# Two transformer stacks on one core: unread transposes ahead of the first product, the first x tile by the scalar queue, the last norm's sums by products, results by two queues

## The chip, the core and the metric

One core of a Trainium2 chip runs the whole program in one launch. The metric is device time in microseconds (us), from three runs. Engines are named as in the profile: PE does matrix products and transposes and writes PSUM banks, PEld is PE's weight load, DVE and ACT do elementwise work, POOL does a little of it, SP only starts transfers. A transfer's data is moved by 16 DMA engines that all queues share; "SPq" and "ACTq" rows are the moments at which SP and ACT issue one.

## What is computed

The program runs two stacks of two layers each over 256 tokens of 1024 features: the first has attention, a short convolution and a gated network per layer, the second has modulated norms, a mixer of three branches and two gated networks per layer. All products are float32. The parts that matter here are the very first product and the very last norm:

```
proj = jnp.einsum('bsd,de->bse', x, w_in)           # the first product, x is [1, 256, 1024]
...
def rms_norm(x, g):                                  # the last operation, over 1024 features
    xf = x.astype(jnp.float32)
    y = xf * lax.rsqrt(jnp.mean(xf * xf, axis=-1, keepdims=True) + EPS)
    return (y * g.astype(jnp.float32)).astype(x.dtype)
```

## The kernel before, in words

Activations lie feature-major: a tile holds two blocks of 128 features by 256 tokens. Each float32 operand is split into a high and a low part, `hi` by ACT (a rounding copy, line 302) and `lo` by DVE (the rest, lines 261 and 305), and a product of two float32 operands is three products on PE, high by high, low by high and high by low (`mm3`, line 373 in `mm`).

**Weights** come as 765 chunks of 512 KB, in the order in which PE uses them (`Weights`). A chunk holds eight 128x128 tiles, so it feeds 8 x 3 = 24 products of 256 columns. It is loaded into one of six `raw` buffers by an SP transfer (line 242), then split by ACT into `wh` and by DVE into `wl`, of which there are six each. A `raw` buffer is free again when DVE has made `wl`. Loads are issued as far ahead as the buffers allow, splits four chunks ahead.

**Start** (`setup`, line 495 on). SP issues in turn the four tiles of x (`x`, 256 KB each) and the first four weight chunks, then the vectors, the distance table and two conditioning rows `cb`. POOL fills `ones768` and builds the identity `ident` that every transpose on PE needs. The transfer of `rope` on ACT's queue is written much later in the program (line 526) but stands first on ACT, because nothing holds it back. A layer under the kernel records the whole program, orders each engine's instructions and sets the waits. It gives transfers eight semaphores in turn, so a ninth transfer is issued when the one eight places earlier has landed.

The first products (`g`, in `mixer1`) run over the feature blocks outermost: chunk 0 uses the first block of x, and eight chunks fill four PSUM banks. Then ACT copies one of those banks out (`qk`), and PE makes attention logits from the copy (`lg`). On ACT, between the splits of the chunks and that copy, stand a table load and the activation of `cb`.

**End** (`block2`, line 1776 on). The last gated network adds into `h[0]` tile by tile. After each tile ACT squares it (`sq`, line 302 from `rms_add`), and the squares of the first seven blocks are added up in one tile `q`; the eighth stays apart as `last`. `rms_root` calls `colsum` (line 476): four transposes on PE put `q` and `last` token-major into a PSUM bank, and DVE adds each row up. Seven small DVE instructions (`rsqrt`) make the inverse root `rs`. Meanwhile ACT multiplies each of the eight blocks with the gain (`hg`), PE transposes each to token-major (`tr`, line 1785), two banks for each half of the tokens. Last, two DVE and two ACT instructions scale the four banks with `rs` into `out` tiles of 256 KB, and SP issues the four result transfers (line 1793).

Of the kernel before, what the change touches and what calls it, by code (L numbers as in the profile page):

```python
# [10 lines left out]
F32 = mybir.dt.float32  # L11
# [4 lines left out]
ALU = mybir.AluOpType  # L16
# [3 lines left out]
P = 128  # L20
D = 1024
# [258 lines left out]
class Kernel:  # L280
# [212 lines left out]
    def setup(self):  # L493
        nc, sb = self.nc, self.sb
        a = self.aps
        self.w = Weights(self, a["w"], self.NSPLIT - 2, 6)

        self.xs_raw = [self.slot("x") for _ in range(4)]
        for j in range(4):
            nc.sync.dma_start(self.xs_raw[j], a["x"][:, 2 * j:2 * j + 2, :])  # L500
            self.w.load(j + 1)
        nv = a["vecs"].shape[1]
        self.vecs = sb.tile([P, nv], F32, name="vecs")
        self.ident = sb.tile([P, P], F32, name="ident")
        self.ones768 = sb.tile([P, P], F32, name="ones768")
        nc.gpsimd.memset(self.ones768, 1.0 / 768)
        make_identity(nc, self.ident)
        nc.sync.dma_start(self.vecs, a["vecs"])
        self.dist = sb.tile([P, 2, 384], F32, name="dist")
        nc.sync.dma_start(self.dist, a["dist"].rearrange("p (a b) -> p a b", a=2))  # L510
        self.rope = sb.tile([P, T], F32, name="rope")
        self.dft_h = sb.tile([P, 768], F32R, name="dft_h")
        self.dft_l = sb.tile([P, 768], F32R, name="dft_l")
        self.cb = sb.tile([P, 2, D], F32, name="cb")
        nc.sync.dma_start(self.cb[:, 0, :], a["c"].partition_broadcast(P))
        nc.sync.dma_start(self.cb[:, 1, :], a["c_ctx"].partition_broadcast(P))
        self.mods = sb.tile([P, DEPTH, 2, NADA], F32, name="mods")
        self.convpad = sb.tile([P, 3, T + 32], F32, name="convpad")
        nc.gpsimd.memset(self.convpad, 0.0)
        self.cpad = [sb.tile([P, T + 2], F32, name=f"cpad{j}") for j in range(2)]  # L520
        for j in range(2):
            nc.gpsimd.memset(self.cpad[j], 0.0)
# [1178 lines left out]
    def block2(self, h_lat):  # L1701
        self.h = [h_lat, None]
        h = self.h
        self.roots = {}
        for l in range(DEPTH):
            last = l == DEPTH - 1
            got = {}
            if l == 0:
                self.rms_all(0)
                us = self.normed(0, 0)  # L1710
                self.ffn_early(3, self.et)
                h[1] = self.load_ctx()
            else:
                self.norm_both(0, 0)
                us = list(zip(*self.u))
                self.u = None
            for s in range(2):
                self.rms_begin(s)

            self.ada_plan(l, 24, 72, ADA[3]) if l else self.ada_plan(l, 24, 72, ADA[4], ADA[5])  # L1720
            if l:
                self.ada_gate(l, 0)

            def ctx_done():
                self.ada_ready(l, 1)
                got["c"] = self.normed(1, 1)

            if l == 0:
                uc, self.uc = self.uc, None
                self.ffn_rest(f"a{l}", us, uc, self.ffn2_add(0, h, (0, 1)), ctx_done)  # L1730
                self.early = None
            else:
                self.ffn_both(f"a{l}", us, self.ffn2_add(0, h, (0, 1)), ctx_done)
            del us

            self.layer_vectors(l)
            def lat_norm():
                got["x"] = self.normed(0, 1)

            if not last:  # L1740
                self.sides.append(self.root_side(0))
                kctx, vctx = self.mixer2(l, 1, got.pop("c"), h[1], None, None, lat_norm)
                rest = lambda: None
            else:
                lat_norm()
                kctx, vctx, rest = self.ctx_keys(l, got.pop("c"))

            def ctx_norm():
                self.u = self.both_operands("u")
                self.norm_both(1, 2)  # L1750

            if not last:
                self.sides.append(self.root_side(1))
            self.mixer2(l, 0, got.pop("x"), h[0], kctx, vctx, (lambda: None) if last else ctx_norm, rest)
            del kctx, vctx, rest
            if not last:
                self.ada_plan(1, 0, 24, ADA[2])
                self.norm_both(0, 2)
                us = list(zip(*self.u))
                self.u = None  # L1760

                def next_ctx():
                    self.ada_ready(1, 0)
                    self.u = self.both_operands("u")
                    self.norm_both(1, 0)

                for s in range(2):
                    self.rms_begin(s)
                self.ffn_both(f"b{l}", us, self.ffn2_add(2, h, (0, 1)), next_ctx)
                del us  # L1770
            else:
                us = self.normed(0, 2)
                add = self.ffn2_add(2, h, (0,))
                self.rms_begin(0)
                self.ffn_single("c", us, 2, lambda m, psum, last: add(0, m, psum, last))
        y = self.rms_root(0, D)
        g = self.vec("g_final_2", 0)
        banks = [[self.bank("mm", "tr") for _ in range(2)] for _ in range(2)]
        for k in range(KD):
            if k % 2 == 0:  # L1780
                t = self.slot("hg")
            self.act(t[:, k % 2, :], h[0][k // 2][:, k % 2, :], AF.Copy, scale=g[:, k:k + 1])
            for b in range(2):
                o = banks[b][k // 4].rearrange("p a b -> p (a b)")[:, (k % 4) * P:(k % 4 + 1) * P]
                self.nc.tensor.transpose(o, t[:, k % 2, b * P:(b + 1) * P], self.ident)
        for j in range(2):
            for b in range(2):
                t = self.slot("out")
                if b:
                    self.act(t, banks[b][j], AF.Copy, scale=y[:, b:b + 1])  # L1790
                else:
                    self.ts(t, banks[b][j], y[:, b:b + 1], None, ALU.mult)
                self.nc.sync.dma_start(self.aps["out"][b * P:(b + 1) * P, j * 512:(j + 1) * 512],
                                       t.rearrange("p a b -> p (a b)"))


# [45 lines left out]
```

## Time and profile before

| | us |
|---|---|
| median of three runs | 2903.86 (2903.77 to 2904.89) |
| the profiled execution, its own time | 2903.97 |
| its span, first to last instruction | 2902.2 |
| outside the span | 1.77 |
| PE busy | 2866.9 (99% of the span) |
| first product starts at | 7.28 |
| first result transfer issued at | 2897.01 |

The profile is one execution. Section 1 of its page gives busy time by engine; the view of waits gives, for each engine, what ended its idle time; the timeline gives start, length, engine, line, operation and operands, with the idle time just before in brackets; the table by stretch gives busy time, granted clock of PE, mean busy share of the DMA engines and GB/s.

### The profile page before, as it was taken

Reading aid. Unit: us, or ns where it says so; the run is one execution under the profiler, and the core shown is the slowest. Engines: PE = TensorE matmul, PEld = TensorE weight load, DVE = VectorE, ACT = ScalarE, POOL = GpSimd, SP = SyncE. Lnnn points to the kernel's source line nnn. Section 1 sums busy time; section 2 is a strip of 40 time slices with the busy share of each in tenths; the row PEclk is TensorE's granted clock in tenths of the full one; section 3 lists DMA queues with packets and bytes.
Section 4 is the critical chain, followed back from the end, with each engine's and each line's share of the span. In section 5 each row is a group of like instructions: output and inputs, shape, how many; then the busy total and the mean of one; then the engine's idle time right before and its main releaser. Section 6 shows DMA issues by size and latency. Waiting matters only on the chain. (4 is left out here: it accounts for less than half of the span.)

```text
span 2902.2 us, 49995 instructions
## 1 busy us (share of the span) xinstructions
PE 2866.9 (99%) x20172; PEld 2648.9 (91%) x20172; DVE 2084.9 (72%) x3565; ACT 1356.8 (47%) x2171; POOL 112.1 (4%) x121
## 2 busy tenths in 40 slices
PE   8999999999999999999999999999999999999999
PEld 7999899899999999999999998888888888899998
DVE  7879778648767787798878875555765556887554
ACT  6645545744554432257557643222322223675443
POOL 1001001000001000010010000000100001000000
PEclk9999999999999999999999999999999999999999
DMA  7565655354654764544453443333354443435452
GB/s 280 195 228 178 221 202 174 133 186 150 210 187 160 240 218 167 172 155 153 165 178 117 153 167 131 138 131 116 114 184 167 167 159 113 162 112 175 160 183 101
DMA packets 134440, 486.30 MB, mean 168 GB/s; under 512 B 14912, under 2 KB 15168, under 8 KB 134208
## 3 DMA queue, kind: packets, MB, share of 16 engines
q1 hardware_dynamic: 133776, 482.58, 48.1%
q8 instruction: 158, 2.59, 0.4%
q14 instruction: 74, 0.61, 0.1%
q10 hardware_dynamic: 432, 0.52, 0.1%
HBM read 482.00 MB, written 1.05 MB: 166 GB/s over the span
## 5 line engine op out<-in xcount | busy, mean ns | idle before, releaser
L302 ACT ACTIVATE wh<-raw 128x1024 fp32r<-128x1024 f32 x765 | 808.1, 1058 | 1127.8 <-issue 180.9
L261 DVE TENSOR_TENSOR wl<-raw,wh 128x1024 fp32r<-128x1024 f32 x765 | 939.3, 1230 | 454.7 <-ACT wh L302 443.1
L547 DVE SCALAR_TENSOR_TENSOR junk<-ada,cb 128x1024 bf16<-128x1024 f32 x256 | 313.4, 1224 | 3.1 <-DMA ada<-in_w_ada_dram 1.1
L373 PE MATMUL f<-x,wh 128*128 128x512 f32 (+1 forms) x832 | 243.4, 359 | 0.0
L373 PE MATMUL f<-x,wl 128*128 128x256 f32 x704 | 185.1, 280 | 0.0
L373 PE MATMUL bg<-wh,wh 128*128 128x256 f32 x576 | 168.0, 292 | 0.0
L373 PE MATMUL bg<-wh,wl 128*128 128x256 f32 x576 | 163.4, 284 | 0.0
L373 PE MATMUL bg<-wl,wh 128*128 128x256 f32 x576 | 162.9, 283 | 0.0
L373 PEld LDWEIGHTS f<-x,wh 128*128 128x128 f32 x832 | 142.9, 188 | 19.7 <-DVE fm L305 0.2
L373 PE MATMUL b<-uh,wl 128*128 128x512 f32 (+1 forms) x384 | 145.8, 380 | 0.0
L373 PE MATMUL a<-uh,wh 128*128 128x512 f32 (+1 forms) x384 | 145.3, 379 | 0.0
L1214 POOL TENSOR_TENSOR sq<-sq,sq 128x256 f32<-128x256 f32 x63 | 64.3, 1028 | 2097.8 <-ACT sq L302 2075.4
L373 PE MATMUL a<-wh,wh 128*128 128x256 f32 x512 | 144.8, 283 | 0.0
L373 PE MATMUL a<-wl,wh 128*128 128x256 f32 x512 | 144.6, 282 | 0.0
L373 PE MATMUL b<-ul,wh 128*128 128x512 f32 (+1 forms) x384 | 144.3, 376 | 0.0
L373 PE MATMUL a<-uh,wl 128*128 128x512 f32 (+1 forms) x384 | 144.2, 376 | 0.0
L373 PE MATMUL a<-ul,wh 128*128 128x512 f32 (+1 forms) x384 | 143.7, 374 | 0.0
L373 PE MATMUL a<-wh,wl 128*128 128x256 f32 x512 | 143.7, 281 | 0.0
L373 PE MATMUL b<-uh,wh 128*128 128x512 f32 (+1 forms) x384 | 143.6, 374 | 0.0
L373 PEld LDWEIGHTS f<-x,wl 128*128 128x128 f32 x704 | 131.8, 187 | 6.2
L308 DVE SCALAR_TENSOR_TENSOR cva<-convpad,wdw,cva 128x256 f32<-128x256 f32 x270 | 126.9, 480 | 3.0
L373 PEld LDWEIGHTS bg<-wh,wh 128*128 128x128 f32 x576 | 108.7, 189 | 4.3 <-issue 4.1
(452 smaller groups left out, 8424.5 us busy)
## 6 DMA issues: line engine op xcount, KB each, us to landing
raw<-in_w_dram SPq DMA_DIRECT2D x765, 512.0 KB, 3.3
ada<-in_w_ada_dram SPq DMA_DIRECT2D x144, 512.0 KB, 4.2
hc<-in_ctx_dram SPq DMA_DIRECT2D x8, 256.0 KB, 5.4
x<-in_x_dram SPq DMA_DIRECT2D x4, 256.0 KB, 5.9
out_dram<-out SPq DMA_DIRECT2D x4, 256.0 KB, 2.4
cb<-in_c_dram SPq DMA_DIRECT2D x1, 512.0 KB, 8.6
cb<-in_c_ctx_dram SPq DMA_DIRECT2D x1, 512.0 KB, 8.2
dist<-in_dist_dram SPq DMA_DIRECT2D x1, 384.0 KB, 7.9
```

Source lines behind the costliest of these rows:

```text
L261: self.last_split = kb.nc.vector.tensor_tensor(lo.rearrange("p a b -> p (a b)"), raw, f.bitcast(F32), ALU.subtract)
L302: return self.nc.scalar.activation(out, in_, func, **kw)
L308: return self.nc.vector.scalar_tensor_tensor(out, a, s, b, op0, op1)
L373: return self.nc.tensor.matmul(out, a, b, start=start, stop=stop)
L547: self.nc.vector.scalar_tensor_tensor(junk, raw, 1.0, self.cb[:, s, :], ALU.mult, ALU.mult, accum_out=self.mods[:, l, s, c:c + 1])
L1214: self.nc.gpsimd.tensor_tensor(r["q"], r["q"], q[:, 0, :], ALU.add)
```

## The change

Four edits, two at each end of the program; the order of everything between is the same on all engines.

1. The first tile of x is issued by ACT, not by SP.
2. POOL makes the identity first, and PE then does 20 transposes of the identity into a bank that is not read.
3. The last norm's sums are made by four products of `q` and `last` (as weights) with a column of ones, which leave the sums of 128 tokens in one column each; DVE's row sum is gone, and the small DVE chain reads PSUM.
4. Of the four result transfers, the two that ACT's `out` tiles feed are issued by ACT.

```diff
         for j in range(4):
-            nc.sync.dma_start(self.xs_raw[j], a["x"][:, 2 * j:2 * j + 2, :])
+            (nc.sync if j else nc.scalar).dma_start(self.xs_raw[j], a["x"][:, 2 * j:2 * j + 2, :])
             self.w.load(j + 1)
...
+        make_identity(nc, self.ident)
+
+        idle = self.bank("st", "idle").rearrange("p a b -> p (a b)")
+        for _ in range(20):
+            nc.tensor.transpose(idle[:, :P], self.ident, self.ident)
         nc.gpsimd.memset(self.ones768, 1.0 / 768)
-        make_identity(nc, self.ident)
+        self.one = sb.tile([P, 1], F32, name="one")
+        nc.gpsimd.memset(self.one, 1.0)
...
-        y = self.rms_root(0, D)
+        r = self.rms.pop(0)
+        st = self.bank("st", "fs")
+        for b in range(2):
+            for j, x in enumerate(("q", "last")):
+                self.mm(st[:, b, 0:1], r[x][:, b * P:(b + 1) * P], self.one, j == 0, j == 1)
+        v = self.small("v")
+        self.ts(v, st[:, :, 0], -1.0 / D, -1e-6, ALU.mult, ALU.add)
+        y = self.rsqrt(v)
...
-                self.nc.sync.dma_start(self.aps["out"][b * P:(b + 1) * P, j * 512:(j + 1) * 512],
+                (self.nc.scalar if b else self.nc.sync).dma_start(self.aps["out"][b * P:(b + 1) * P, j * 512:(j + 1) * 512],
```

PE's instructions at the start. `g` is the bank of the first products, `xh` and `xl` the parts of x, `wh` and `wl` those of chunk 0. Before:

```order
L373 MATMUL g_17_125<-xh_101,wh_135 128x256
L373 MATMUL g_17_125<-xl_102,wh_135 128x256
L373 MATMUL g_18_126<-xh_101,wh_135 128x256
L373 MATMUL g_18_126<-xl_102,wh_135 128x256
L373 MATMUL g_19_127<-xh_101,wh_135 128x256
L373 MATMUL g_17_125<-xh_101,wl_136 128x256
```

After:

```order
L510 MATMUL idle_84<-ident 128x128 x20
L373 MATMUL g_18_148<-xh_124,wh_158 128x256
L373 MATMUL g_18_148<-xl_125,wh_158 128x256
L373 MATMUL g_18_148<-xh_124,wl_159 128x256
L373 MATMUL g_18_148<-xh_124,wh_158 128x256
L373 MATMUL g_18_148<-xl_125,wh_158 128x256
```

The first product that needs `wl` stood sixth; it now stands third, behind the transposes and two products.

ACT's instructions at the start, with the letters as above and `x` the tile as loaded. Before:

```order
L526 DMA rope<-in_rope_dram 128x256
L302 ACT_TABLE_LOAD
L302 ACTIVATE xh_101<-x_61 128x512
L302 ACTIVATE wh_135<-raw_66 128x1024
L302 ACTIVATE xh_105<-x_62 128x512
```

After:

```order
L500 DMA x_61<-in_x_dram 128x512
L532 DMA rope<-in_rope_dram 128x256
L302 ACT_TABLE_LOAD
L302 ACTIVATE xh_124<-x_61 128x512
L302 ACTIVATE wh_158<-raw_66 128x1024
L302 ACTIVATE xh_128<-x_62 128x512
```

The x tile stands ahead of `rope` on ACT; on SP every transfer of the start stands one place earlier.

ACT's last instructions. `tr` are the transposed banks, `rs` the inverse root. Before:

```order
L302 ACTIVATE hg_31607<-r_8742,vecs 128x256 x2
L302 ACTIVATE hg_31614<-r_8743,vecs 128x256 x2
L302 ACTIVATE hg_31621<-r_8744,vecs 128x256 x2
L302 ACTIVATE out_31631<-tr_31598,rs_31587 128x512
L302 ACTIVATE out_31637<-tr_31599,rs_31587 128x512
```

After:

```order
L302 ACTIVATE hg_31635<-r_8766,vecs 128x256 x2
L302 ACTIVATE hg_31642<-r_8767,vecs 128x256 x2
L302 ACTIVATE out_31652<-tr_31619,rs_31608 128x512
L302 ACTIVATE out_31658<-tr_31620,rs_31608 128x512
L1806 DMA out_dram<-out_31652 128x512
L1806 DMA out_dram<-out_31658 128x512
```

Both of ACT's result transfers stand behind both of its `out` instructions; SP keeps the two of DVE's tiles.

## Rows read from the trace of the kernel before

**Rows 1.** Section 1 of the page: span; busy time of the engines.
```profile
span 2902.2 us, 49995 instructions
PE 2866.9 (99%) x20172; PEld 2648.9 (91%) x20172; DVE 2084.9 (72%) x3565; ACT 1356.8 (47%) x2171; POOL 112.1 (4%) x121
```
**Rows 2.** Waits of PE: us in total, times, longest us.
```profile
PE g L373 <- ACT wh L302: 7.3, 1, 7.3
...
PE lg L373 <- ACT qk L302: 1.1, 1, 1.1
```
**Rows 3.** Timeline of the start: start us, us, engine, line, operation.
```profile
0.71 0.42 ACTq L526 DMA_DIRECT2D rope<-in_rope_dram  x1
...
0.72 0.38 SPq L500 DMA_DIRECT2D x<-in_x_dram  x1
...
1.15 0.42 SPq L242 DMA_DIRECT2D raw<-in_w_dram  x1
...
1.85 0.29 POOL masks.py:199 TENSOR_SCALAR_AFFINE_SELECT ident<-ident 128x128 f32<-128x128 f32 x1
...
4.82 0.63 ACT L302 ACTIVATE xh<-x 128x512 fp32r<-128x512 f32 x1 [2.37 <-DMA x<-in_x_dram]
...
6.17 1.06 ACT L302 ACTIVATE wh<-raw 128x1024 fp32r<-128x1024 f32 x1 [0.72 <-DMA raw<-in_w_dram]
...
7.26 1.31 DVE L261 TENSOR_TENSOR wl<-raw,wh 128x1024 fp32r<-128x1024 f32 x1 [1.09 <-ACT wh L302]
```
**Rows 4.** PE's products (line 373) by stretch: busy (count), PEclk, DMA share, GB/s.
```profile
7.28:10.65 3.37, 3.37 (x15) 3.17 (x15) 1.00 1.03 412
10.65:13.53 2.88, 2.88 (x27) 2.88 (x26) 1.00 1.04 409
```
**Rows 5.** ACT's timeline between the chunk splits and the copy for `lg`.
```profile
27.75 1.06 ACT L302 ACTIVATE wh<-raw 128x1024 fp32r<-128x1024 f32 x1 [0.21 <-DMA raw<-in_w_dram]
28.83 1.28 ACT L302 ACT_TABLE_LOAD   x1
30.12 1.92 ACT L302 ACTIVATE cb<-cb 128x2048 f32<-128x2048 f32 x1
...
32.89 0.58 ACT L302 ACTIVATE qk<-g 128x512 f32<-128x512 f32 x1
```
**Rows 6.** PE's timeline at the logits `lg`.
```profile
33.52 0.93 PE L373 MATMUL lg<-qk,qk 64*128 64x128 f32 x8 [1.14 <-ACT qk L302]
```
**Rows 7.** By stretch: PE, PEld, DVE, ACT, POOL busy, PEclk, DMA share, GB/s.
```profile
1.50:3.50 2.00, 0.00 (x0) 0.00 (x0) 0.00 (x0) 0.94 (x1) 1.12 (x4) 1.00 0.43 123
3.50:33.52 30.02, 25.10 (x195) 24.66 (x195) 19.06 (x21) 19.59 (x21) 6.16 (x4) 1.00 1.02 403
```
**Rows 8.** Timelines of the end.
```profile
2892.94 3.29 ACT L302 ACTIVATE hg<-r,vecs 128x256 f32<-128x256 f32 x8
...
2893.09 0.55 PE L482 MATMUL cs<-ident,sq 128*128 128x128 f32 x3 [0.92 <-ACT sq L302]
2893.49 3.23 PE L1785 MATMUL tr<-ident,hg 128*128 128x128 f32 x16
...
2893.67 0.69 DVE L484 TENSOR_REDUCE cs<-cs 128x2 f32<-128x512 f32 x1 [1.09 <-PE cs L482]
...
2895.97 0.16 DVE L308 SCALAR_TENSOR_TENSOR rs<-rt,rs 128x2 f32<-128x2 f32 x1
...
2896.22 1.27 ACT L302 ACTIVATE out<-tr,rs 128x512 f32<-128x512 f32 x2
2896.24 1.41 DVE L312 TENSOR_SCALAR out<-tr,rs 128x512 f32<-128x512 f32 x2
2897.01 1.81 SPq L1793 DMA_DIRECT2D out_dram<-out  x4
```
**Rows 9.** By stretch at the end, columns as in rows 7.
```profile
2897.01:2897.87 0.86, 0.00 (x0) 0.00 (x0) 0.63 (x1) 0.48 (x1) 0.00 (x0) 1.00 0.02 10
2897.87:2900.62 2.75, 0.00 (x0) 0.00 (x0) 0.00 (x0) 0.00 (x0) 0.00 (x0) 0.56 1.01 376
```
**Rows 10.** Transfers by queue: KB each, median us from issue to landing.
```profile
dft<-in_dft_dram ACTq DMA_DIRECT2D x1, 256.0 KB, 4.2
...
out_dram<-out SPq DMA_DIRECT2D x4, 256.0 KB, 2.4
```

## The prediction

> **What bounds the kernel now.** I read the page's busy times first. PE is busy for 99% of a span of 2902.2 us [rows 1], so nothing but PE's own work or PE's idle time can matter, and all four edits stand in the first 34 us and the last 10. The view of waits comes next: PE's longest wait is the 7.3 us before its first product, and some 26 us later it waits 1.1 us once more, at the logits `lg` [rows 2]. That second wait is the one to see: a microsecond won before it is only kept if whatever ends that wait also comes earlier.
>
> The timelines tell what ends it. PE starts `lg` at 33.52, after 1.14 us idle, when ACT has copied `qk` [rows 6]. ACT reaches that copy at 32.89, out of an unbroken row of work: a chunk split at 27.75, a table load, the activation of `cb`, one more split, the copy [rows 5]. The split at 27.75 waited for its weight chunk, for a transfer and not for PE. The table by stretch shows why: from 3.5 us to 33.5 us the DMA engines are busy all the time (share 1.02, 403 GB/s), and only the 2.0 us from 1.5 to 3.5 run low, at 123 GB/s [rows 7]. So the first 33 us go at the pace of the transfers. PE has 1.14 us to spare at the logits.
>
> At the end the timelines show a similar thing. ACT scales eight `hg` blocks from 2892.94 to 2896.23 and only then comes to its `out` tiles; the transposes `tr` follow it until 2896.72; DVE has `rs` at 2896.13, just in time [rows 8]. From 2897.87 to 2900.62 the four results flow without a gap (share 1.01) [rows 9].
>
> **The change part by part.** The sum is made against the profiled execution, 2903.97 us (span 2902.2, 1.77 outside it), which lies 0.11 above the median of 2903.86 and inside the three runs.
>
> *x by ACT.* SP issues x at 0.72 and the first weight chunk at 1.15; ACT issues `rope` at 0.71 [rows 3]. Now x takes `rope`'s place on ACT, `rope` goes about 0.4 later, and every SP transfer of the start moves up one place, 0.43 us. The ACT table load behind the two issues moves from 1.16 to some 1.6, and x isn't there until 4.82, so that costs nothing. What the stream of transfers gains is at most what lies idle in its slow beginning. If all SP transfers just come 0.43 earlier, all landings do, the one at 27.75 too, and with it `qk`, `lg` and the rest of the program. If x and the first chunk now share the engines and nothing starts moving sooner, the gain is 0. The landing of x may itself fall back, since it shared with nothing but `rope` before: by at most 0.64 us, the time of 256 KB at 403 GB/s [rows 7]. Then `xh` and, behind it on ACT, `wh` come later, but this delays only PE's first product, not the stream. I take 0.35, nearer to the upper end, because SP was issuing x, chunk and x in turn, one behind another, just before the stream filled. Bounds: a loss of 0.2 (SP's later issues wait for landings of the earlier ones, x among them) and a gain of 0.6.
>
> *Unread transposes.* PE waits in any case until `wh` of chunk 0 is there. The identity was ready at 2.14 [rows 3]; now that it is built ahead of a 0.82 us fill it may be ready at about 1.5 to 2.1. Three transposes with the identity took 0.55, and one lasts about 0.27, so one follows another after 0.14 at the end of the program, with the clock at its upper level [rows 8]. At the lower level I double that: 20 take 2.8 to 5.6 us, and end between 4.5 and 7.7, so at the worst 0.8 after the first product could begin (6.9). What they could win is seen in the first products. Before, fifteen take the 3.37 us up to 10.65, one per 0.22, and from there on a chunk's 24 take 2.88, one per 0.12 (the table counts each product that overlaps a stretch) [rows 4]. The spacing nearly halves, from one level of 1.2 GHz to the other of 2.4, after some 3 us of products (the granted clock of the table reads 1.00 throughout, so it is the spacing that tells).
>
> With the clock up from the first product PE would gain this: the first product that needs `wl` of chunk 0 starts when DVE has it, at 8.57 before [rows 3] and 0.43 less in the best case, about 8.2. It now stands third, not sixth, and the sixteenth follows 13 x 0.12 later, at 9.76, where it stood at 10.65: 0.89 us won. With the clock low PE loses up to 0.4. Neither reaches `lg`: a win lengthens the 1.14 us wait there, a loss shortens it. So I cost this edit at 0, hidden by ACT's row of work from 27.75 on. Without this cover it would be worth between -0.89 and +0.4.
>
> This case's rows show no transposes ahead of products, so they can't tell whether these raise the clock. The Trainium skill, "TensorE: Matmul & The Clock Gate", Part 4, speaks against it: transposes do not count as activity for the clock in the way products do. By that the edit would bring the loss of 0.4 rather than the win of 0.89; under the wait at `lg` the sum is the same by both.
>
> *Sums by products.* Out goes DVE's row sum, 0.69 + 0.02 us of the chain to `rs` [rows 8]. Three transposes behind the last square took 0.55; three float32 products take their place. The nearest float32 products are `lg`: eight rows for four instructions, next to each other, in 0.93 [rows 6]. So three, with two rows each, take 0.7 to 0.9 us, 0.15 to 0.35 more. `rs` comes 0.35 to 0.55 earlier, at about 2895.7. What that releases is only DVE's first `out` tile, since the bank is long transposed: 2895.7 to 2896.45. Everything else waits for ACT's `hg` row and the transposes behind it, which do not move.
>
> *Results by two queues.* The first result flowed 0.86 us after its issue (2897.01 to 2897.87) and one takes 2.75 / 4 = 0.69 us [rows 9]. Now the first, issued at about 2896.45, flows from 2897.3 to 2898.0. DVE's second tile can't start before the last transposes at 2896.7, is done at 2897.45 and flows from 2898.3. ACT's two tiles end at 2897.49 [rows 8]; both its transfers stand behind both, and are issued at about 2897.5 and 2897.95, to flow from 2898.4 and 2898.8. Three results from 2898.3 on end at 2898.3 + 3 x 0.69 = 2900.35, where 2900.62 was the end: -0.3. Bounds: 0 if ACT's issue is slower, -0.6 if all of DVE's gain arrives; the other side is a rival below.
>
> The sum: -0.35 + 0 - 0.3 = -0.65, so 2903.97 - 0.65 = 2903.3 us, with a range of its own from 2902.8 (-0.6 - 0.6) to 2904.2 (+0.2 and 0).
>
> **The rivals.**
>
> *The slow beginning is filled.* If two queues fill the 2.0 us at 123 GB/s, 0.25 MB that need 0.6 us at 403 GB/s, the stream moves up by up to 1.4 us [rows 7]. With PE's 1.14 spare and its 0.89, `lg` could follow in full: -1.4 - 0.3, 2902.3; without a higher clock `lg` follows by 1.14 at most (or less by the 0.4): 2902.5. For it speaks that low stretch; against it that `rope` on ACT's queue and x on SP's were under way together already then [rows 3], so two queues alone did not fill it, and I give it a small chance. The Trainium skill, "DMA: Bandwidth & Descriptors", section "Issuing engines are not separate DMA queues", says that transfers of all issuers run on the same engines and a second issuer saves only issuing time. By that the start gains no more than the issue slot of 0.43, and the sum stays at 2903.3.
>
> *Nothing moves at the start.* x and the first chunk share the engines, the landing at 27.75 stays, and only the end gains: 2903.97 - 0.3 = 2903.7. Against it: each SP issue does come earlier.
>
> *Slower: ACT's results land late.* The one transfer of 256 KB on ACT's queue in the trace took 4.2 us from issue to landing, SP's results 2.4 [rows 10]. If the last one, issued at 2897.95, takes 4.2, it lands at 2902.15; SP's last, issued at about 2898.4, landed by 2.4 at some 2900.8. That is +1.35, with the start's -0.35: 2905.0. It decides against the change from 3.2 us to landing on. Against it: ACT's 4.2 was a load among weight transfers, the results are stores with the engines to themselves.
>
> **How the numbers follow.** Forecast 0.58; the slow beginning filled 0.12; nothing at the start 0.18; slower by ACT's queue 0.10; anything else 0.02. All four cases lie within 1.7 us of the profiled execution before. What a measurement of this kernel can tell from no change is about 0.2%, 5.8 us, so they all count as the same, 0.96 after a bit is kept for what I don't see on either side (0.02 each). The range leaves out most of the slower rival and the end of the first one: 2902.4 to 2904.4.
>
> **What would show it.** Right: the wait before the first product a few tenths under 7.3; the wait at `lg` longer than 1.14, by about what PE wins in the first products; `qk` and the splits some 0.35 earlier; `rs` near 2895.3 (0.35 and 0.45 earlier) and no DVE row sum; a gap between the first result and the other three. A spacing of the first products of 0.12 would show the clock up, one of 0.2 the lower level. Wrong: `lg` released by something other than ACT's copy, the split that was at 27.75 earlier by a microsecond or later, or a last landing more than 3.2 us after an ACT issue.

## The result, and the profile of the changed kernel

The changed kernel takes 2864.1 us (median of four runs, 2863.29 to 2866.85), the kernel before 2904.37 in the runs beside it: a ratio of 0.9862, with an interval from 0.985 to 0.9874. The change saves 40 us, 1.4%, clear of the spread of both kernels (the four runs before lie from 2903.77 to 2904.89). The forecast was 2903.3, from 2902.4 to 2904.4.

Page of the changed kernel, section 1, which answers to [rows 1]:
```profile
span 2862.8 us, 50040 instructions
...
PE 2827.9 (99%) x20196; PEld 2620.8 (92%) x20196; DVE 2082.8 (73%) x3564; ACT 1355.5 (47%) x2171; POOL 114.0 (4%) x122
```
PE is busy for 39.0 us less than before (2866.9) with 24 matrix instructions more, and idle for as long (34.9 against 35.3). DVE and ACT work as long as they did. So PE did the same products faster.

Where it does so can be read from two stretches in the middle of the run, where no edit stands. The first holds products of 256 columns (called narrow below), the second products of 512 (wide). By stretch, PE alone, first the kernel before, then the changed one; columns: busy time (products that overlap the stretch), PEclk, DMA share, GB/s:
```profile
1110.00:1130.00 20.00, 20.00 (x169) 1.00 0.53 180
1850.00:1870.00 20.00, 20.00 (x87) 1.00 0.39 136
```
```profile
1110.00:1130.00 20.00, 20.00 (x172) 1.00 0.45 161
1850.00:1870.00 20.00, 20.00 (x89) 1.00 0.29 108
```
PE is full in all four, at a granted clock of 1.00, and yet more products fit in: 172 of 256 columns in place of 169, 89 of 512 in place of 87. The spacing, that is the mean time from the start of a product to the next start, over all steady pairs in the trace (100 to 140 ns apart for 256 columns, 205 to 260 for 512), fell from 119.9 to 117.5 ns and from 233.2 to 229.6. There are 15314 products of the first kind and 3696 of the second: 15314 x 2.4 + 3696 x 3.6 ns = 50 us. Some 10 come back at the joints, where gaps are longer than these; 40 remain.

The start, in the changed kernel's timeline, answers to [rows 3, 5, 6]:
```profile
1.45 4.53 PE L510 MATMUL idle<-ident 128*128 128x128 f32 x20 [1.45 <-POOL ident masks.py:199]
...
5.36 0.63 ACT L302 ACTIVATE xh<-x 128x512 fp32r<-128x512 f32 x1 [2.44 <-DMA x<-in_x_dram]
...
6.99 0.58 PE L373 MATMUL g<-xh,wh 128*128 128x256 f32 x1 [1.02 <-ACT wh L302]
...
13.54 0.30 PE L373 MATMUL g<-xh,wl 128*128 128x256 f32 x1
...
27.85 1.06 ACT L302 ACTIVATE wh<-raw 128x1024 fp32r<-128x1024 f32 x1 [0.21 <-DMA raw<-in_w_dram]
...
32.99 0.58 ACT L302 ACTIVATE qk<-g 128x512 f32<-128x512 f32 x1
...
33.00 0.28 PE L373 MATMUL g<-xh,wl 128*128 128x256 f32 x1
...
33.62 0.93 PE L373 MATMUL lg<-qk,qk 64*128 64x128 f32 x8
```
x lands 0.54 us later (told by the start of ACT's `xh`, which waits for it). The split of the chunk at 27.75, `qk` and `lg` come 0.10 later. The wait at `lg` is gone, since PE's last product `g` ahead of it starts at 33.00, where it started at 31.87 in the kernel before:
```profile
31.87 0.28 PE L373 MATMUL g<-xh,wl 128*128 128x256 f32 x1
```
The end answers to [rows 8]:
```profile
2853.10 0.48 DVE L308 SCALAR_TENSOR_TENSOR r<-cd,hg,r 128x256 f32<-128x256 f32 x1 [0.66 <-PE cd L373]
...
2854.09 0.83 PE L373 MATMUL fs<-one,sq 128*128 128x1 f32 x6 [0.91 <-ACT sq L302]
...
2856.51 0.16 DVE L308 SCALAR_TENSOR_TENSOR rs<-rt,rs 128x2 f32<-128x2 f32 x1
2856.78 1.62 DVE L312 TENSOR_SCALAR out<-tr,rs 128x512 f32<-128x512 f32 x2
...
2857.13 1.31 ACT L302 ACTIVATE out<-tr,rs 128x512 f32<-128x512 f32 x2
...
2857.56 1.21 SPq L1806 DMA_DIRECT2D out_dram<-out  x2
2857.83 1.01 ACTq L1806 DMA_DIRECT2D out_dram<-out  x2
```
From the last `r` (2853.10) to the end of the span it is 9.70 us, where it was 10.10 (2892.10 to 2902.2). By these two profiles both ends together (0.10 lost, 0.40 won) are worth 0.3 us of the 40.

### The profile page after: what moved, and what is told of

It is laid out like the page before. It is cut to its first block, busy times and chain, and to the rows that moved or that the text cites. A ratio compares the mean times of both kernels' runs of the same rounds, so it can differ in the third digit from the quotient of the medians.

```text
span 2862.8 us, 50040 instructions
## 1 busy us (share of the span) xinstructions
PE 2827.9 (99%) x20196; PEld 2620.8 (92%) x20196; DVE 2082.8 (73%) x3564; ACT 1355.5 (47%) x2171; POOL 114.0 (4%) x122
```

## The experiments

The edits have a side effect that reaches the middle: they move tiles. `one` is 4 bytes of each partition and takes 32. All tiles allocated behind it start 32 bytes later: the built program has the six `wh` tiles from byte 146464 of each partition before and from 146496 after, the `wl` tiles 24576 bytes behind them in both. The activation slots (x, `xh`, `xl` and all others), from 1152 on, and `raw` stay. So the first theory (A in the expectations) was: the place of the weight tiles sets PE's spacing, a multiple of 64 bytes as in the changed kernel being good and 32 off one bad. Its rival (B): the edits do, by the clock or by the phase in which the products begin. What turned out to count is a third thing, the distance from the slots to the weight tiles, taken modulo 256 bytes: 160 before, 192 after.

**A pad and no edit.** The kernel before with an unread tile where `one` stands:
```diff
         make_identity(nc, self.ident)
+        self.pad = sb.tile([P, 1], F32, name="pad")
+        nc.gpsimd.memset(self.pad, 1.0)
```


> The kernel before with one thing added: a tile of 128x1 f32 (4 bytes of each partition, 32 reserved), set once by POOL and read by nobody, allocated where the changed kernel has its tile `one`. Every tile behind it, wh and wl among them, starts 32 bytes later: wh and wl at a multiple of 64 bytes, where they stood 32 off one. Theory A (the place of the weight tiles in SBUF sets PE's spacing): 2864 to 2866 us, 39 to 40 below the kernel before, with the 256-column products 0.1177 us apart instead of 0.120. Theory B (the edits at the start and the end set it, by the clock or by the phase in which the products begin): 2904, as before. A mixture would lie between.

Measured: 2864.91 us, ratio 0.9861 (0.9846 to 0.9876). The pad alone gives the whole gain, with the spacings of the changed kernel (117.5 and 229.6). The rival falls. PE alone, by stretch:
```profile
1110.00:1130.00 20.00, 20.00 (x172) 1.00 0.49 160
1850.00:1870.00 20.00, 20.00 (x89) 1.00 0.34 125
```

**All edits and the old residue modulo 64.** The changed kernel with `one` 64 bytes wide (distance 224):
```diff
-        self.one = sb.tile([P, 1], F32, name="one")
+        self.one = sb.tile([P, 16], F32, name="one")
```


> The changed kernel with its tile `one` 16 columns wide in place of 1 (64 bytes; column 0 is the one that the products read), so that wh and wl stand 32 bytes off a multiple of 64 again, as in the kernel before; every edit stays. Theory A (place in SBUF): the 39 us are gone; 2903 to 2905, and what is left against the kernel before, within 0.7 us, is the sum of the edits at the two ends (+0.1 and -0.44 by the profiles: -0.35). Theory B (the edits): 2864, as the changed kernel.

Measured: 2869.62, ratio 0.9878 (0.9863 to 0.9893). It is neither of the two expectations: the residue modulo 64 is that of the kernel before, and most of the gain stays. The theory of a multiple of 64 falls. PE alone, by stretch:
```profile
1110.00:1130.00 20.00, 20.00 (x174) 1.00 0.49 172
1850.00:1870.00 20.00, 20.00 (x87) 1.00 0.39 135
```
The 256-column products are closer than in the changed kernel, the 512-column ones as far apart as before. Each of the two kinds has its own good places.

**Only wl moved.** The kernel before with the pad between `wh` and `wl`:
```diff
             hi = kb.sb.tile([P, 8, P], F32R, tag="wh", bufs=kb.NSPLIT, name=f"wh{c}")
+            if c == 0:
+                kb.pad = kb.sb.tile([P, 1], F32, name="pad")
+                kb.nc.gpsimd.memset(kb.pad, 1.0)
             lo = kb.sb.tile([P, 8, P], F32R, tag="wl", bufs=kb.NSPLIT, name=f"wl{c}")
```


> The kernel before with a tile of 128x1 f32 (32 bytes reserved) between the wh tiles and the wl tiles: wh stays 32 bytes off a multiple of 64, wl moves to a multiple of 64. Of the three products of a split pair two read wh and one reads wl. Theory A, a price per product that reads a displaced weight tile: a third of the 39 us comes, 2890 to 2893. If it is not PE's reading but another engine's write of the weights that counts (ACT writes wh, DVE writes wl), the gain is near all or near nothing: about 2865 or 2904. Theory B (the edits): 2904.

Measured: 2879.9, ratio 0.9914 (0.9897 to 0.993). No expectation holds: it is not a third, nor all, nor nothing. The 256-column products are 117.9 ns apart, the 512-column ones 233.0. So there is no price per product that reads a displaced tile: moving `wl`, which one of three products reads, speeds up all three of the narrow kind (117.2 to 118.3 ns, by the kind of step, from 119.5 to 120.3) and none of the wide.

**All tiles moved together.** The kernel before with the pad ahead of the slots.
```diff
+        self.pad = sb.tile([P, 1], F32, name="pad")
         self.w = Weights(self, a["w"], self.NSPLIT - 2, 6)
```


> The kernel before with the 32 bytes put ahead of all tiles: wh and wl stand at a multiple of 64 as in the changed kernel, but the slots `s` (x, xh, xl and all other activations, the other operand of every product), raw and vecs now stand 32 bytes off one, where they stood at a multiple in both kernels. Theory A with the weight tiles alone: 2864 to 2866. Theory A2, each of PE's two operands that starts off a multiple of 64 costs its own price: the weights' 39 us come and the activations cost as much or more, 2895 to 2935. Theory B (the edits): 2904.

Measured: 2904.94, ratio 1.0001 (0.9992 to 1.0011); 119.9 and 233.2 ns, as before. `wh` and `wl` stand where the changed kernel has them, and nothing is won, since the slots moved along. What counts is a distance between tiles, not a place.

**The slots stay, raw moves with the weights.** The pad stands between the slots and `raw`:
```diff
         self.xs_raw = [self.slot("x") for _ in range(4)]
+        self.pad = sb.tile([P, 1], F32, name="pad")
```


> The kernel before with the 32 bytes between the activation slots and everything behind them: raw, vecs, ident, wh, wl and the rest move by 32 bytes together, the slots stay. The first four runs showed that no residue of 64 decides (moving the weights by 64 bytes keeps nearly the whole gain, moving all tiles together by 32 gains nothing), so a distance between two tiles does. Theory D1, the distance from the activation slots to the weight tiles, PE's two operands: 2864 to 2866, as with the pad behind ones768. Theory D2, the distance from raw to wh and wl (a read of ACT or DVE, or a landing, against a write beside it): raw and the weights keep their distance, so 2903 to 2906, as before.

Measured: 2864.81, ratio 0.9862 (0.9833 to 0.989). It is the distance from the slots to the weights, PE's two operands, not the one from `raw`.

**Products alone, by distance.** The function that builds the kernel is replaced by products, 48 at each distance for 256 columns (`x` holds eight slots, `w` the two parts of the weights, from which `wh` and `wl` are cut at the distance; two rounds of eight pieces):
```diff
+        x = sb.tile([P, 8, 512], F32R, name="x")
+        w = sb.tile([P, 2, 6144], F32R, name="w")
+                    nc.tensor.matmul(o[:, :256], wh, xh, start=first, stop=False)
+                    nc.tensor.matmul(o[:, :256], wh, xl, start=False, stop=False)
+                    nc.tensor.matmul(o[:, :256], wl, xh, start=False, stop=last)
```


> Products alone, nothing else of the computation (the output is filled with ones): 48 products of 256 columns or 24 of 512 for each of 64 distances between the two operands' tiles, 0 to 2016 bytes by 32, in the order of the kernel before (weight high by activation high, high by low, low by high; steps of 512 bytes in the weights), no engine or DMA beside them; then 16 pairs of distances for the two parts of the weights. The kernel before has the distance 1952 modulo 2048, the changed one 1984, the one with the wide tile 2016. Theory D1, PE's two reads meet in SBUF by their distance: 119.9 ns from one 256-column product to the next at 1952, 117.5 at 1984, 117.0 at 2016; 233.2, 229.6 and 233.0 for 512 columns; a pattern that repeats with the distance, and perhaps a better one than any so far. Theory D2, PE meets other engines' or the DMAs' accesses: one and the same spacing at all distances, at or below the smallest seen.

No other engine is busy during these products. In the timeline of this run the first products at the distances 160 (`naf`), 192 (`nag`), 224 (`nah`) and 256 (`nba`):
```profile
55.74 0.28 PE L1821 MATMUL naf<-x,w 128*128 128x256 f32 x1
...
61.49 0.28 PE L1821 MATMUL nag<-x,w 128*128 128x256 f32 x1
...
67.14 0.28 PE L1821 MATMUL nah<-x,w 128*128 128x256 f32 x1
...
72.81 0.28 PE L1821 MATMUL nba<-x,w 128*128 128x256 f32 x1
```
48 products lie between two of these rows: 119.8, 117.7 and 118.1 ns each, the step to the next distance included. Over all 64 distances the mean spacing within a group repeats every 256 bytes to 0.1 ns (first line: distance modulo 256; the very first group of each kind, up to 2 ns longer, is left out):
```
                          0     32     64     96    128    160    192    224
256 columns, ns       119.8  118.3  117.8  117.4  118.6  119.8  117.8  117.8
512, weights moving   227.7  233.4  229.3  233.9  233.5  234.1  233.5  233.1
```
With no other engine and no transfer at work, the narrow products show the spacings of the full kernels: 119.8 at 160 (the kernel before: 119.9), 117.8 at 192 (the changed one: 117.5). So the distance between PE's two operands modulo 256 bytes sets the spacing with no other engine's help, as theory D1 has it, and D2 falls. The second line doesn't fit the kernels (229.6 at 192); the reason stands under "The other wide products".

**The distance 64.** The changed kernel with `one` 160 bytes wide (`[P, 40]`):

> The changed kernel with `one` 40 columns wide (160 bytes): the distance from the activation slots to the weight tiles is 64 modulo 256 in place of 192. By the spacings of products alone at each distance (117.8 ns for 256 columns at both, 229.3 against 233.5 for 512) and 15314 and 3696 products: 2864 - 15 = 2849 us, if the two spacings hold beside the other engines. By the spacings that the changed kernel itself shows at 192 (117.5 and 229.6) nothing is left to gain at 64: 2864 to 2869. A distance that has no effect beyond the one of the first theory (any but 160 is as good) gives the same 2864 to 2869.

Measured: 2853.03 (2848.53 to 2859.74), ratio 0.9815 (0.9799 to 0.9831). Better than the changed kernel by 11 us, but not where it was expected (in the wide products). The profile is of the run at 2859.74:
```profile
1110.00:1130.00 20.00, 20.00 (x179) 1.00 0.52 167
1850.00:1870.00 20.00, 20.00 (x87) 1.00 0.35 120
```
179 narrow products, 113 ns each (each lasts 0.28 us, so 20.28 us hold the 179), below anything in the table; the wide ones are back at 87. Over this whole trace the narrow mean is 115.7, since other stretches stand at 117.8.

**Without the transposes, and with x by SP.** The changed kernel less one start edit each:
```diff
-        for _ in range(20):
-            nc.tensor.transpose(idle[:, :P], self.ident, self.ident)
```


> The changed kernel without the 20 unread transposes; all else as in it, `one` and the distance 192 too. If the transposes are what makes the first products start 0.3 us earlier, but the clock rise later (about 13.5 us in place of 10.5) and the product that waits for attention's lg come no earlier: the first product at 7.2 to 7.3, the products 0.215 us apart until 10 to 11 us, lg again waiting for ACT, and lg at 33.5 to 33.6. If the queue of x decides the start, lg stays at 33.6. Whole time: as the changed kernel, 2862 to 2867, since a tenth of a microsecond can't be told from its runs.


```diff
-            (nc.sync if j else nc.scalar).dma_start(self.xs_raw[j], a["x"][:, 2 * j:2 * j + 2, :])
+            nc.sync.dma_start(self.xs_raw[j], a["x"][:, 2 * j:2 * j + 2, :])
```


> The changed kernel with the first x tile issued by SP as before; all else as in it. If ACT's queue is what made x land at 5.36 in place of 4.82 and all loads behind it 0.1 us later: x lands at 4.8 to 4.9, ACT's row of work is 0.1 us earlier and lg at 33.5. If the later landing comes of something else (the transposes' or the allocation's), x lands at 5.3 again. Whole time as the changed kernel, 2862 to 2867.

Measured: 2857.86 (two runs, 2851.08 and 2864.64), ratio 0.9837 (0.9809 to 0.9865); 2858.24 (2854.08 and 2862.41), 0.9838 (0.9818 to 0.9858). One program with one distance gave two times 13.6 us apart, and neither median lies in the range that was expected (2862 to 2867). In the profile of the run at 2851.08 the stretch from 1100 to 1120 us holds 179 products, at the distance 192 at which the changed kernel has 172 there:
```profile
1100.00:1120.00 20.00, 20.00 (x179) 1.00 0.53 174
```
So the distance is not all. The closer spacing holds without a break from 960 us to 1220 us and is gone behind that. First the changed kernel (its run at 2864.57), then this one:
```profile
960.00:1220.00 260.00, 260.00 (x2209) 1.00 0.58 199
960.00:1220.00 260.00, 260.00 (x2297) 1.00 0.62 204
```
88 products more, at 117.8 ns each, are 10 of the 13.5 us between these two runs. The profile with x by SP (2854.08) shows the same stretch with 2296.

The start without the transposes:
```profile
7.07 0.58 PE L373 MATMUL g<-xh,wh 128*128 128x256 f32 x1 [7.07 <-ACT wh L302]
...
33.78 0.93 PE L373 MATMUL lg<-qk,qk 64*128 64x128 f32 x8 [1.65 <-ACT qk L302]
```
The first product starts at 7.07, nearer to the 6.99 with transposes than to the 7.28 before, so they are not what lets it start earlier. The products are 0.21 us apart until 10.20 and `lg` waits for ACT again, both as expected. The start with x by SP:
```profile
4.37 0.63 ACT L302 ACTIVATE xh<-x 128x512 fp32r<-128x512 f32 x1 [1.93 <-DMA x<-in_x_dram]
...
6.79 0.38 PE L373 MATMUL g<-xh,wh 128*128 128x256 f32 x1 [0.81 <-ACT wh L302]
...
34.50 0.71 PE L373 MATMUL lg<-qk,qk 64*128 64x128 f32 x6 [1.90 <-ACT qk L302]
```
Issuing it from ACT does make x land later: `xh` starts at 5.30 to 5.44 in all six profiles with it, at 4.25 to 4.82 in all six without. But `lg` is no earlier for an early x (34.50 here, where 33.5 was expected).

**Finer steps.** Products alone, the low part of the activation moved too, and distances by 4 bytes:

> Products alone as in the run with 64 distances: the output filled with ones, nothing else computed. Now the low part of the activation lies 0 to 224 bytes by 32 off the place it has in the kernels, for each distance of the weights 0 to 224; then the distances of the weights by steps of 4 bytes from 0, 64 and 192. If PE reads lines of 32 bytes or more and only the line counts, steps of 4 bytes inside one line leave the spacing alone or add one step; if the exact distance counts, the spacing changes with each. If the low part's own distance counts as the weights' does, the table of 8 by 8 shows its own good and bad places, and perhaps one below 117.4 and 227.7 ns, the least seen.

The low part's own place counts as well: with it 128 off, 160 gives 118.2 ns in place of 120.1. Steps of 4 bytes count, so the exact distance does and not a line of 32 bytes: from 64 on, 113.8, 118.3, 118.3, 113.3 ns at 64, 68, 72, 76. And 64 gave 117.8 in the first such run, in all eight of its groups.

**The other wide products.** Only 288 of the 3696 wide products have the weights moving; the others hold 128x128 of weights and move a whole slot:
```diff
+                nc.tensor.matmul(o, wh, xh, start=k == 0, stop=False)
+                nc.tensor.matmul(o, wh, xl, start=False, stop=False)
+                nc.tensor.matmul(o, wl, xh, start=False, stop=k == 7)
```


> Products alone once more (output filled with ones, nothing else computed). The runs before had, as 512-column products, those with the weights moving, which are 288 of the kernel's 3696; the others hold 128x128 of the weights and move a whole slot of 512 columns. Here these: 24 for each distance 0 to 252 bytes by 4, first upward and then downward, and 24 of 256 columns for the same distances, upward and downward. Theory D1: 512 columns give 233 ns at 160, 229.6 at 192, 233 at 224 and at 64, as the kernels with these distances did. If the distance alone decides, upward and downward agree at each; if what went before decides among two or more steady spacings, they differ at some (256 columns at 192: 117.8 and 113.4 were both seen in runs of the kernel).

The wide ones now fit the kernels: 233.5 ns at 160, 228.9 at 192, 233.2 at 224 and 64 (kernels: 233.2, 229.6, 233.0, 233.2). They are closest at 0, 226.7 upward and 226.6 downward. The narrow ones at 192, first upward (`nga`, then `ngb`), then downward (`rga`, then `rfh`), 24 products each:
```profile
162.93 0.28 PE L1821 MATMUL nga<-x,w 128*128 128x256 f32 x1
...
165.76 0.28 PE L1821 MATMUL ngb<-x,w 128*128 128x256 f32 x1
...
251.17 0.28 PE L1821 MATMUL rga<-x,w 128*128 128x256 f32 x1
...
253.89 0.28 PE L1821 MATMUL rfh<-x,w 128*128 128x256 f32 x1
```
2.83 us upward, 2.72 downward: 117.9 and 113.3 ns at one distance. At 64 it is 113.3 upward and 117.8 downward. At 76 both give 113.4, at 180 113.4 and 113.3 (means of what repeats, without the first products at a distance). Elsewhere the two can lie further apart: wide products at 156 settle at 226.7 upward and 243.3 downward, and narrow ones at 28 at 133.3 in the run before and at about 117 from both sides here. So at some distances PE has more than one steady spacing, and which one it takes goes with what ran before.

**Each piece of weights at its own distance.** The changed kernel with wider weight tiles; the pieces (chunks of 512 KB) of the wide products (WIDE, ranges of their numbers) at 0, all others at 76 (a start at column 35) or at 180 (61):
```diff
-            hi = kb.sb.tile([P, 8, P], F32R, tag="wh", bufs=kb.NSPLIT, name=f"wh{c}")
-            lo = kb.sb.tile([P, 8, P], F32R, tag="wl", bufs=kb.NSPLIT, name=f"wl{c}")
+            o = 16 if any(i <= c < j for i, j in WIDE) else 35
+            hi, lo = (kb.sb.tile([P, 1088], F32R, tag=t, bufs=kb.NSPLIT, name=f"{t}{c}")[:, o:o + 1024]
+                      .rearrange("p (a b) -> p a b", a=8) for t in ("wh", "wl"))
```


> The changed kernel with wider weight tiles (1088 columns, of which 1024 are used) so that each piece of weights stands at a chosen distance from the activation slots: 0 modulo 256 for the pieces whose products have 512 columns (WIDE), 76 for all others, in place of 192 for all. Products alone gave 226.7 ns for 512 columns at 0 and 113.4 for 256 at 76, both from either side, against 229.6 and 117.5 in the changed kernel. Theory D1 with the spacing settled by distance: 15314 x 4.1 + 3696 x 2.8 ns = 73 us less, about 2791 us. If the kernel's other orders of products (steps between banks, keys and values) or the spacings kept from what went before decide as much: 2810 to 2850. If only 32-byte places are good for ACT's and DVE's writes: longer wh and wl rows (1058 and 1231 ns before), and the time near or above 2864.

> As the kernel with 76 and 0, with 180 in place of 76 for the 256-column pieces. Products alone gave 113.4 and 113.3 ns there from the two sides. Theory D1 settled by distance: the same 2791 us as with 76, within 5. If what products alone show at a distance is no guide inside the kernel, the two differ by more than that, and either may lie near 2864.

Measured: 2819.23 (2813.95 to 2829.01), ratio 0.9706 (0.9685 to 0.9727) with 76; 2846.48 (2844.55 to 2855.19), 0.9794 (0.9777 to 0.981) with 180. The first beats both kernels, by 87 and 45 us, and lies in the range that was given to other orders of products or kept spacings (2810 to 2850); the second differs from it by 27 us where 5 were allowed. The page and stretches of the first, then the stretches with 180:
```profile
span 2816.1 us, 50040 instructions
...
PE 2770.1 (98%) x20196; PEld 2567.1 (91%) x20196; DVE 2081.9 (74%) x3564; ACT 1354.9 (48%) x2171; POOL 114.1 (4%) x122
```
```profile
1110.00:1130.00 20.00, 20.00 (x179) 1.00 0.55 185
1850.00:1870.00 20.00, 20.00 (x90) 1.00 0.42 140
```
```profile
1110.00:1130.00 20.00, 20.00 (x172) 1.00 0.46 154
1850.00:1870.00 20.00, 20.00 (x90) 1.00 0.33 116
```
The wide products come within 1.2 ns of what they showed alone in both (227.6 and 227.9). The narrow ones do so at 76 (113.9 ns) and not at 180 (117.3); but this profile with 180 is of the slowest of its runs, 2855.19, and no trace shows whether the three faster ones have more of the closer spacing. With 76 the spacings are worth 15314 x 3.6 + 3696 x 2.0 = 62 us against the changed kernel, and 45 arrive: PE's idle time grew from 34.9 to 46.0 us. Many waits on DVE and ACT grew a little; the wait at `lg` is 2.4 us, and the two largest in total are these (columns: total us, times, longest; first the changed kernel):
```profile
PE cs L482 <- DVE sq L305: 5.9, 4, 2.5
PE rsb L490 <- DVE rs L308: 4.9, 7, 2.5
```
```profile
PE cs L486 <- DVE sq L309: 7.3, 5, 2.9
PE rsb L494 <- DVE rs L312: 5.6, 9, 2.6
```

## Why the prediction was wrong

**The step that failed** stands in its first sentences: all four edits stand in the first 34 us and the last 10, and so only these can change. The premise was right (PE's own work bounds the kernel) and the conclusion not. The tile `one` was costed as three products' operand and nothing else; that it shifts all tiles behind it by 32 bytes, and with them one operand of 19000 products, was no term of the sum and no rival. The runs showed this in its place: the spacing fell from 119.9 to 117.5 ns and from 233.2 to 229.6 over the whole run, and the same shift by a pad, without any of the edits, gave 2864.91 us. The range of 2 us could not hold a cause that acts at each product. The 0.02 kept for "anything else" was the only place for it.

The priced terms, each by its own step:

*x by ACT*, -0.35: no gain is seen, and a size can't be shown. By one of the prediction's own signs the term failed: the split at 27.75 came later, at 27.85. Its bound on the other side came true in part: x lands later, by 0.54 us in the profile, near the 0.64 allowed. The slow stretch of the beginning moved faster (from 1.50 to 3.50, 201 to 226 GB/s in the six profiles with x by ACT, 123 to 199 in the six with x by SP), and still nothing reached `lg`: it starts at 33.47 to 34.44 in the five profiles with the old start, at 33.62 to 34.72 in the five with both edits. The rival in which the slow beginning is filled and the stream follows by 1.4 us is not seen. The Trainium skill, "DMA: Bandwidth & Descriptors", section "Issuing engines are not separate DMA queues", gave this second issuer at most its issuing time; the trace agrees as far as these 12 profiles tell.

*Unread transposes*, 0, hidden by ACT's row: right in `lg`, with two surprises ahead of it. They took 4.53 us, inside the 2.8 to 5.6 of the estimate. In the changed kernel's own profile the low level then lasted longer: 256-column products are 0.21 us apart until 13.54, where it was 10.50 before and 10.2 to 11.7 in the other five without transposes. So PE's last product ahead of `lg` came 1.13 us later, not by the 0.4 at most that the prediction allowed, and that the 1.14 of spare time just covered it was luck. But in the other five profiles with transposes ahead the first product is at the upper level already (0.38 or 0.39 us long, against 0.58 in all six without transposes and in this one), and in four of these five it stays there; in the fifth it fell back after the wait for `wl`, until 11.17. The granted clock reads 1.00 in these stretches, so it is the spacing and the length that tell. The rule of the Trainium skill that the prediction weighed ("TensorE: Matmul & The Clock Gate", Part 4: transposes don't count as products do) agrees with one profile and disagrees with five, and the measurement decides: mostly they do bring the level up. Why one profile differs stays open. What the upper level wins is lost at `lg`, as costed: PE waits there for ACT's `qk` for 1.21 to 1.90 us in the four, for 1.09 to 2.00 in the six without transposes, so that not even a longer wait stands out.

*Sums by products and two queues*, -0.3: the sign and nearly the size hold, the mechanism in part. Three products in six rows took 0.83 (0.7 to 0.9 expected); from the last `r` to the end of `rs` it is 3.57 us, where it was 4.03, so 0.46 less (0.35 to 0.55 expected). The end of the span follows by 0.40: 9.64 to 9.70 us behind the last `r` in the changed kernel and six variants of it, 10.05 to 10.10 in the kernel before and four of its own. The gap behind the first result, which the prediction worked out from ACT's transfers standing behind both `out` instructions, didn't come: ACT issued its first one at 2857.83, when the first `out` was done and the second still ran. All four flow from 2858.40 on:
```profile
2858.40:2861.18 2.78, 0.00 (x0) 0.00 (x0) 0.00 (x1) 0.05 (x1) 0.00 (x0) 0.84 1.00 374
```
*Slower by ACT's queue*: its results landed 2.8 us after their issue, under the 3.2 from which that rival decided:
```profile
out_dram<-out SPq DMA_DIRECT2D x2, 256.0 KB, 2.5
out_dram<-out ACTq DMA_DIRECT2D x2, 256.0 KB, 2.8
```

What stays open: which of two spacings PE takes at a distance that has both, and with it what sets off the stretch of 260 us that makes most of the 13 us between two runs, and why 180 is good for products alone and less so in the kernel's profile. That the distance between PE's two operands acts is shown (no other engine is needed, and the places of both operands count). That their two reads get in each other's way is the likely reason, but no view shows it.

## What to carry to other kernels

In this kernel a new tile of 4 bytes moved all tiles that are allocated behind it, and 32 bytes were worth 1.4% and well-chosen distances 3%. Where PE is full, read the spacing of its products in the middle of the run before and after any change, even one at the ends: if it differs, look at addresses first, and give the old kernel the same shift with a pad before you credit the edit. To tune it, measure products alone over the distances between the two operands, for each shape and from both sides, and then in the kernel, since of the two places tried one kept its promise. One profile can mislead here: a run can hold either spacing for hundreds of microseconds, so look at several runs and at the whole trace.

## What the runs showed of the hardware

- With no other engine at work, the spacing of products depends on the distance between the held and the moving operand in SBUF, with a period of 256 bytes: 117.4 to 119.8 ns by 32-byte steps for 256 columns, 226.6 to 234.2 for 512; single 4-byte steps move it by as much (113.3 to 118.3 between 64 and 76).
- At some distances there are two steady spacings, 113.3 and 117.8 ns at 192 and at 64 (256 columns), and which one holds goes with what came before. Two runs of one kernel were 13.6 us apart; in the faster one, which was profiled, the closer spacing held for 260 us, worth some 10 us.
- Behind 20 unread transposes the first product was at the upper of the clock's levels in five of six profiles (0.38 or 0.39 us long, against 0.58), without them in none of six.
- A load of 256 KB issued by ACT beside SP's landed later than the same load issued first by SP: the copy that waits for it started at 5.30 to 5.44 us, against 4.25 to 4.82.
